# Layer A's normed queries turned in 32×32 blocks by VectorE, with a head every five slots

## The chip, the core and the metric

The kernel runs on one core of a Trainium2 chip. Its engines are TensorE (PE in the profile, with its weight loads as PEld), VectorE (DVE), ScalarE (ACT), GpSimd (POOL) and SyncE (SP, which only issues DMAs). Each works through its own instructions in a fixed order and waits at an instruction until the semaphores it needs have come. The metric is the device time of one execution in microseconds (us), the median of several runs.

## What is computed

A two-layer encoder over 256 tokens of width 2048: layer A has banded softmax attention with normed queries and keys, layer B another attention; both have a cross-attention into 256 memory tokens, an output projection and an MLP. The change lies in layer A's projections and attention:

```python
xn = rms_norm(h, norm_attn[layer])
mem_n = rms_norm(mem, norm_mem[layer])
proj = xn @ w_in_a[layer]
q = rms_norm(split_heads(proj[..., :W_MAIN], N_HEADS_MAIN), qk_gain_a[layer, 0])
k = rms_norm(split_heads(proj[..., W_MAIN:2 * W_MAIN], N_HEADS_MAIN), qk_gain_a[layer, 1])
v = split_heads(proj[..., 2 * W_MAIN:3 * W_MAIN], N_HEADS_MAIN)
y_main = chunk_band_attention(q, k, v, rel_bias[layer])
qm = proj[..., 3 * W_MAIN:]
y_mem = memory_attention(split_heads(qm, N_HEADS_MEM), mem_n, w_mem_kv[layer],
                         qk_gain_mem[layer, 0], qk_gain_mem[layer, 1])
```

There are 12 banded heads and 4 memory heads, each 128 wide. A query or key is divided by its own root mean square, and multiplied by a gain that has one value per feature of the head. The scores are products of queries and keys, so a gain of the queries may as well be put on the keys.

## The kernel before

**Numbers in halves.** Every weight is split into a high part that TensorE can multiply fast (`hi`, made by ScalarE, L173) and the remainder (`lo`, made by VectorE, L176). A *unit* is 1024 columns of weights for 128 partitions: one DMA into `raw`, one `hi`, one `lo`. There are 6 buffers for `raw`, 4 for `hi` and 5 for `lo`, and `weights()` prepares units up to three ahead of the one TensorE uses. A new `hi` can therefore begin when TensorE has finished the unit four before it.

**Groups and slots.** In layer A `tokens_major` computes a block of 512 output columns for all 256 tokens: 8 units of 12 matmuls, into two PSUM banks (one for each half of the tokens). After every unit it calls `slot()`, which lets each active side job take one step, up to its next `yield`. The matmuls and transposes a side job issues there stand in TensorE's order between two units, because TensorE's instructions are kept in the order in which the program writes them. On the other engines the build's scheduler decides the order. So TensorE's place for a head's work is fixed by slots, and what VectorE does before that head's work is fixed by the scheduler.

**The order of the groups.** Layer A has ten groups: `qm` (the four memory heads' queries), then three times `q`, `k`, `v` for four banded heads each, called here q0, k0, v0, q1, … v2. That is 80 slots; with slot 0 at the end of `qm`, q0 ends at slot 8, k0 at 16, v0 at 24, q1 at 32, k1 at 40, v1 at 48, q2 at 56, k2 at 64, v2 at 72.

**Norming and turning** (`normed_heads`, L556). For each of a group's two halves: ScalarE squares the bank (`sqw`, L561), VectorE sums the squares (`ss`, L563) and scales them (`msq`, L567), GpSimd takes the power −1/2 (`sroot`, L571), VectorE multiplies the bank by it (`qn`, L573). `qn` has tokens on the partitions, but the scores need the head's features there. So after `wait` slots TensorE transposes four blocks of 128×128 against an identity into the PSUM tile `tp`, and ScalarE copies `tp` to the destination with the gain as its scale (L592); one half in each of two slots. All queries and keys go this way.

**Heads.** `queue_side` puts a head in a line that is first in, first out: a head starts no earlier than 5 slots after it was queued, and no earlier than `gap` slots after the head before it. Memory heads have a gap of 4, banded heads of 2 (the last four: 1). A memory head (`mem_head`, L641) does its score matmuls `s`, the maximum (`nmax`, L651), the exponentials (`p`, L657) and their reciprocal sums (`rs`) in its first slot's step; four slots later it transposes `p` on TensorE into `tp`, ScalarE copies that to `pt`, and two slots later comes `yp`, the product with the values. A banded head (`band_head`, L667) loads its bias in its first slot, does `s`, `ns` (VectorE, L684), the exponentials (ScalarE, L692), `rs` (L697) and the scaling of `ns` (VectorE, L617, 128 and then 256 columns) in the second, transposes `ns` two slots after that, and multiplies by the values one slot later. `split_psum` then writes `y` (ScalarE L473, VectorE L474).

With these gaps the memory heads start at slots 5, 9, 13, 17, and the banded heads at 21, 23, 25, 27, then 45, 47, 49, 51, then 69 to 72. A banded head's `s` comes one slot after its start.

**Stages.** Memory keys and values come first, then layer A's ten groups (about 90 to 345 us), the output projection, the MLP, and layer B.

Of the kernel before, what the change touches and what calls it, by code (L numbers as in the profile page):

```python
# [9 lines left out]
F32 = mybir.dt.float32  # L10
# [6 lines left out]
P = 128  # L17
# [88 lines left out]
def trunk(  # L106
# [161 lines left out]
    def start_side(g):  # L268
        active.append(g)

    def queue_side(g, gap):
        waiting.append((g, gap, clock["slot"] + 5))

    def slot():
        clock["slot"] += 1
# [179 lines left out]
    def pin(ins, pinned=True):  # L455

        if pinned:
            tc.keep_in_program_order(ins)
# [88 lines left out]
    def inverse_square(acc, name):  # L547
# [5 lines left out]
        nc.vector.reciprocal(r2[:], r2[:])  # L553
        return r2

    def normed_heads(banks, eps_ms, gain, dst, wait=2):  # L556


        def half(m):
            sq = wide.tile([P, 512], F32, name="sqw", tag="wide")  # L560
            nc.scalar.activation(sq[:], banks[m][:], AF.Square)  # L561
            ss = tiny.tile([P, 4], F32, name="ss", tag="t4", bufs=8)
            nc.vector.tensor_reduce(  # L563
                ss[:], sq[:].rearrange("p (h d) -> p h d", d=HD), AX.X, ALU.add
            )
            ms = tiny.tile([P, 4], F32, name="msq", tag="t4", bufs=8)
            nc.vector.tensor_scalar(  # L567
                ms[:], ss[:], 1.0 / HD, eps_ms[:, 2 * m : 2 * m + 1], op0=ALU.mult, op1=ALU.add
            )
            s = tiny.tile([P, 4], F32, name="sroot", tag="t4", bufs=8)  # L570
            nc.gpsimd.tensor_tensor(s[:], ms[:], neg_half[:], op=ALU.pow)  # L571
            qn = wide.tile([P, 512], F32, name="qn", tag="wide")
            nc.vector.tensor_tensor(  # L573
                qn[:].rearrange("p (h d) -> p h d", d=HD),
                banks[m][:].rearrange("p (h d) -> p h d", d=HD),
                s[:].unsqueeze(2).to_broadcast([P, 4, HD]),
                op=ALU.mult,
            )
            return qn

        def side():
            qns = [half(0), half(1)]
            for _ in range(wait):
                yield
            for m in range(2):
                yield
                tp = ps_t.tile([P, 512], F32, name="tp", tag="t")
                for j in range(4):
                    nc.tensor.transpose(
                        tp[:, j * P : (j + 1) * P], qns[m][:, j * P : (j + 1) * P], ident[:]  # L590
                    )
                nc.scalar.activation(  # L592
                    dst.rearrange("p (h t) -> p h t", t=T)[:, :, m * P : (m + 1) * P],
                    tp[:].rearrange("p (h t) -> p h t", t=P),
                    AF.Copy,
                    scale=gain,
                )

        g = side()
        next(g)  # L600
        start_side(g)
# [288 lines left out]

    gq = const.tile([P, 3], F32, name="gq")

    def scale_gains():
        for i in range(3):
            g = sm[:, G_QK + 2 * i : G_QK + 2 * i + 1]
            pin(nc.vector.tensor_scalar_mul(gq[:, i : i + 1], g, QSCALE))

    later(scale_gains, 10)

# [12 lines left out]
    for l, mg in enumerate((mg0, mg1)):  # L912
        if l == 1:
            xg = new_act("xg")
            start_side(
                delayed(spaced(lambda kt: split_scaled(xg, kt, xs(kt), G_ATTN0, True), KT, 1), 4)
            )
        k_ = heads4(f"km{l}")
        km.append(k_)
        vm.append(heads4(f"vm{l}"))  # L920
        g = G_QK + 2 * (1 + l) + 1

        def keys(b, wait, k_=k_, g=g):

            late = 2 + wait
            later(lambda: normed_heads(b, mstat["em"], sm[:, g : g + 1], k_[:], late), wait)

        if l == 0:
            first_two(
                mg,  # L930
                lambda b: later(lambda: value_heads(b, mstat["r"], vm[0]), 5),
                lambda b: keys(b, 2),
            )
            xs = load_tokens(x_t, "xc", nc.sync)
            x_sq = square_sum("x_sq")
            start_side(delayed(all_squares(x_sq, lambda c: xs(4 * c, 4), 1, True), 10))
        else:
            tokens_major(mg, lambda b: keys(b, 0))
            tokens_major(mg, lambda b: value_heads(b, mstat["r"], vm[1]))
# [269 lines left out]

    start_side(x_stat_side())  # L1210
    qm = heads4("qm0")
    tokens_major(xg, lambda b: normed_heads(b, mstat["xem"], gq[:, 1:2], qm[:]))
    y = new_act("y0")
    for j in range(NM):
        queue_side(mem_head(qm, km[0], vm[0], j, y, 2), 4)

    for i in range(3):
        q_, k_, v_ = heads4(f"q{i}"), heads4(f"k{i}"), heads4(f"v{i}")
        tokens_major(xg, lambda b: normed_heads(b, mstat["xem"], gq[:, 0:1], q_[:]))
        tokens_major(  # L1220
            xg, lambda b: normed_heads(b, mstat["xem"], sm[:, G_QK + 1 : G_QK + 2], k_[:])
        )
        ready = {}
        for j in range(4):
            queue_side(band_head(q_, k_, v_, j, 4 * i + j, y, ready, 1), 2 if i < 2 else 1)

        def values(b, v_=v_, ready=ready):
            value_heads(b, mstat["xr"], v_)
# [153 lines left out]
```

## Time and profile before

| | |
|---|---|
| median of 3 runs | 2172.17 us (2171.57 to 2173.44) |
| the profiled execution | 2173.2 us, of which its span 2171.3 us |
| granted TensorE clock | 0.999 |
| DVE busy over the span | 1639.0 us (75%) |
| ACT busy over the span | 1196.6 us (55%) |
| POOL busy over the span | 324.4 us (15%) |
| HBM read and written | 190 GB/s over the span |

The page counts an engine as busy while an instruction of it runs, so a share near 100% means that it hardly ever stood still. It does not say that its work was all needed. The chain of waits is followed back from the last instruction: an engine's share of it is the part of the span that a cut on that engine could shorten.

### The profile page before, as it was taken

The numbers are of one execution on the slowest core, as the hardware profiler recorded it, in microseconds if no ns is written. First come the engines' busy times: TensorE is split into PE (matmuls) and PEld (weight loads), VectorE is DVE, ScalarE is ACT, GpSimd is POOL, SyncE is SP. The second block draws the span as 40 slices with busy tenths as digits, with TensorE's granted clock in tenths as the row PEclk, the third lists the DMA queues.
The fourth block names the chain that finished last, engine by engine and source line by source line (L and its number), as shares of the span: only waits on it lengthen the run. The fifth ranks groups of instructions, "written<-read, shape, count | busy, mean of one in ns | idle before, by whom it ended". The sixth has DMA issues, their size and how long they took to land.

```text
span 2171.3 us, 30203 instructions
## 1 busy us (share of the span) xinstructions
PE 2164.1 (100%) x11123; PEld 1856.6 (86%) x11123; DVE 1639.0 (75%) x2239; ACT 1196.6 (55%) x1680; POOL 324.4 (15%) x349
## 2 busy tenths in 40 slices
PE   9999999999999999999999999999999999999999
PEld 8888888888888888888878888888888888888887
DVE  7765555677977987997876556567797798799796
ACT  7645545555655565555545447655565556555553
POOL 0010102621001001001041112253100100100100
PEclk9999999999999999999999999999999999999999
DMA  9655656665765765666666654455676567667664
GB/s 331 194 173 162 180 173 196 187 193 168 210 214 172 210 210 184 192 214 192 200 177 186 182 192 140 130 185 184 181 207 216 172 198 221 191 178 221 187 182 155
DMA packets 213315, 414.64 MB, mean 191 GB/s; under 512 B 13232, under 2 KB 144304, under 8 KB 213168
## 3 DMA queue, kind: packets, MB, share of 16 engines
q1 hardware_dynamic: 212592, 410.63, 62.3%
q8 instruction: 87, 1.43, 0.3%
q10 hardware_dynamic: 576, 2.10, 0.3%
q14 instruction: 60, 0.49, 0.1%
HBM read 410.58 MB, written 2.10 MB: 190 GB/s over the span
## 4 chain that ended last, share of the span: by engine, by line
PE 99%; DVE 0%; DMA 0%; ACT 0%; issue 0%; ACTq 0%
PE acc L77 94%; PE accs L77 1%; PE tp L77 1%; PE yp L77 1%; PE s L77 1%; PE z L77 1%; DMA raw<-in_w_o 0%; PE cold L77 0%; ACT hi L173 0%; DVE lo L250 0%; DVE h L983 0%; DVE lo L176 0%; DVE kvx L465 0%; ACT hi L249 0%; PE stat L77 0%
## 5 line engine op out<-in xcount | busy, mean ns | idle before, releaser
L176 DVE TENSOR_TENSOR lo<-raw,hi 128x1024 fp32r<-128x1024 f32 (+1 forms) x524 | 644.4, 1237 | 357.6 <-ACT hi L173 239.5
L173 ACT CAST hi<-raw 128x1024 fp32r<-128x1024 f32 (+1 forms) x524 | 546.7, 1045 | 380.0 <-PE acc L77 307.5
L77 PE MATMUL acc<-hi,hid 128*128 128x512 f32 x1474 | 482.4, 390 | 0.0
L77 PE MATMUL acc<-mlpx,hi 128*128 128x512 f32 x2048 | 472.6, 390 | 0.0
L77 PEld LDWEIGHTS acc<-mlpx,hi 128*128 128x128 f32 x2048 | 382.0, 188 | 77.8
L77 PEld LDWEIGHTS acc<-hi,hid 128*128 128x128 f32 x1474 | 277.4, 188 | 57.7
L77 PE MATMUL acc<-lo,hid 128*128 128x512 f32 x737 | 287.4, 390 | 0.0
L1080 POOL TENSOR_TENSOR hid<-upsq,hid 128x256 fp32r<-128x256 f32 x128 | 122.2, 963 | 1086.2 <-ACT hid L1079 1086.2
L227 ACT CAST hi<-raw 128x1024 fp32r<-128x1024 f32 x204 | 192.0, 946 | 132.8 <-PE acc L77 57.2
L77 PEld LDWEIGHTS acc<-mlpx,lo 128*128 128x128 f32 x2048 | 250.6, 192 | 2.8
L77 PE MATMUL acc<-mlpx,lo 128*128 128x256 f32 x2048 | 252.0, 283 | 0.0
L228 DVE TENSOR_TENSOR lo<-raw,hi 128x1024 fp32r<-128x1024 f32 x204 | 222.8, 1107 | 29.3 <-ACT hi L227 27.7
L249 ACT CAST hi<-raw 128x1024 fp32r<-128x1024 f32 x146 | 154.0, 1055 | 127.5 <-PE acc L77 104.0
L77 PE MATMUL acc<-hi,xg 128*128 128x512 f32 x640 | 210.5, 399 | 0.0
L250 DVE TENSOR_TENSOR lo<-raw,hi 128x1024 fp32r<-128x1024 f32 x146 | 178.4, 1222 | 16.3 <-ACT hi L249 15.6
L77 PEld LDWEIGHTS acc<-lo,hid 128*128 128x128 f32 x737 | 138.7, 188 | 28.7
L77 PEld LDWEIGHTS acc<-hi,xg 128*128 128x128 f32 x640 | 120.2, 188 | 24.6
L451 ACT COPY low<-acc 128x256 f32<-128x256 f32 x188 | 69.1, 368 | 112.5 <-PE acc L77 112.2
L77 PE MATMUL acc<-lo,xg 128*128 128x512 f32 x320 | 124.7, 390 | 0.0
L77 PE MATMUL acc<-y,hi 128*128 128x512 f32 x512 | 119.9, 391 | 0.0
L77 PEld LDWEIGHTS acc<-y,hi 128*128 128x128 f32 x512 | 95.0, 188 | 19.1
L1079 ACT CAST hid<-upsq 128x256 fp32r<-128x256 f32 x128 | 51.9, 406 | 77.1 <-DVE upsq L1078 77.1
(200 smaller groups left out, 2570.5 us busy)
## 6 DMA issues: line engine op xcount, KB each, us to landing
raw<-in_w_up SPq DMA_DIRECT2D x256, 512.0 KB, 4.4
raw<-in_w_down SPq DMA_DIRECT2D x256, 512.0 KB, 5.6
raw<-in_w_in SPq DMA_DIRECT2D x80, 512.0 KB, 3.6
raw<-in_w_o SPq DMA_DIRECT2D x64, 512.0 KB, 3.9
raw<-in_w_mem SPq DMA_DIRECT2D x28, 512.0 KB, 6.2
raw<-in_w_kv_v SPq DMA_DIRECT2D x24, 512.0 KB, 3.7
raw<-in_w_kv_k SPq DMA_DIRECT2D x24, 512.0 KB, 4.0
raw<-in_w_q SPq DMA_DIRECT2D x24, 512.0 KB, 4.2
```

Of the source, the lines that this page charges most:

```text
L77: return self._tc.keep_in_program_order(fn(*args, **kwargs))
L173: nc.scalar.copy(hi[:, :n], raw[:, :n])
L176: nc.vector.tensor_tensor(lo, raw, hi.bitcast(F32), op=ALU.subtract)
L227: nc.scalar.copy(hi4, src)
L228: nc.vector.tensor_tensor(lo4, src, hi4.bitcast(F32), op=ALU.subtract)
L249: nc.scalar.copy(hi4, turned)
L250: nc.vector.tensor_tensor(lo4, turned, hi4.bitcast(F32), op=ALU.subtract)
L451: nc.scalar.copy(low[:], bank[:, T:])
L1079: nc.scalar.copy(hid[:, f, :T], a[:])
L1080: nc.gpsimd.tensor_tensor(hid[:, f, T:], a[:], hid[:, f, :T].bitcast(F32), op=ALU.subtract)
```

## The change

Layer A's `qm`, q0, q1 and q2 are no longer transposed by TensorE. A new function `quadrants` lets VectorE turn them in blocks of 32×32: each instruction takes 32 partitions and one block of 32 columns of each of the four heads (32×4×32 elements), turns every block in itself and writes it to the 32 partitions where it belongs. A half needs 16 of them, four in each of four slots, so a group needs 32 over 8 slots. `wait` goes from 2 to 1 for these groups, so their first turn is issued in the slot in which the group ends. The gain of the queries is no longer a scale of the copy; it is multiplied into the keys' gain (`gk`, made from `gq` and the keys' gain by two small VectorE instructions at the start), which the keys' copy uses as before. Keys, and layer B's queries, are still transposed by TensorE.

The heads are spread: memory heads have a gap of 5 and start no earlier than 11 slots after they are queued (`first`), the first eight banded heads have a gap of 5; the last four keep 1. By the rule above, memory heads now start at slots 11, 16, 21, 26, banded heads at 31, 36, 41, 46, then 51, 56, 61, 66, then 69 to 72.

```diff
-    def queue_side(g, gap):
-        waiting.append((g, gap, clock["slot"] + 5))
+    def queue_side(g, gap, first=5):
+        waiting.append((g, gap, clock["slot"] + first))
...
+    def quadrants(qn, m, dst):
+
+
+        src = qn.rearrange("p (h d) -> p h d", d=HD)
+        dst = dst.rearrange("p (h t) -> p h t", t=T)
+        for a in range(4):
+            for b in range(4):
+                nc.vector.transpose(
+                    dst[32 * b : 32 * b + 32, :, m * P + 32 * a : m * P + 32 * a + 32],
+                    src[32 * a : 32 * a + 32, :, 32 * b : 32 * b + 32],
+                )
+            yield
+
     def normed_heads(banks, eps_ms, gain, dst, wait=2):
...
             for _ in range(wait):
                 yield
+            if gain is None:
+                for m in range(2):
+                    yield from quadrants(qns[m][:], m, dst)
+                return
             for m in range(2):
...
+    gk = const.tile([P, 2], F32, name="gk")
+
     def scale_gains():
         for i in range(3):
             g = sm[:, G_QK + 2 * i : G_QK + 2 * i + 1]
             pin(nc.vector.tensor_scalar_mul(gq[:, i : i + 1], g, QSCALE))
+        for i in range(2):
+            k = sm[:, G_QK + 2 * i + 1 : G_QK + 2 * i + 2]
+            pin(nc.vector.tensor_tensor(gk[:, i : i + 1], gq[:, i : i + 1], k, op=ALU.mult))
...
-            later(lambda: normed_heads(b, mstat["em"], sm[:, g : g + 1], k_[:], late), wait)
+            gain = gk[:, 1:2] if k_ is km[0] else sm[:, g : g + 1]
+            later(lambda: normed_heads(b, mstat["em"], gain, k_[:], late), wait)
...
-    tokens_major(xg, lambda b: normed_heads(b, mstat["xem"], gq[:, 1:2], qm[:]))
+    tokens_major(xg, lambda b: normed_heads(b, mstat["xem"], None, qm[:], 1))
     y = new_act("y0")
     for j in range(NM):
-        queue_side(mem_head(qm, km[0], vm[0], j, y, 2), 4)
+        queue_side(mem_head(qm, km[0], vm[0], j, y, 2), 5, 11)
...
-        tokens_major(xg, lambda b: normed_heads(b, mstat["xem"], gq[:, 0:1], q_[:]))
-        tokens_major(
-            xg, lambda b: normed_heads(b, mstat["xem"], sm[:, G_QK + 1 : G_QK + 2], k_[:])
-        )
+        tokens_major(xg, lambda b: normed_heads(b, mstat["xem"], None, q_[:], 1))
+        tokens_major(xg, lambda b: normed_heads(b, mstat["xem"], gk[:, 0:1], k_[:]))
         ready = {}
         for j in range(4):
-            queue_side(band_head(q_, k_, v_, j, 4 * i + j, y, ready, 1), 2 if i < 2 else 1)
+            queue_side(band_head(q_, k_, v_, j, 4 * i + j, y, ready, 1), 5 if i < 2 else 1)
```

The change adds lines ahead of most of the code, so the same instruction has a higher line number: by 14 in the first part of `normed_heads` (`ss` goes from L563 to L577, `qn` from L573 to L587), by 18 behind it (`ns` from L684 to L702, the scaling from L617 to L635). The turns themselves are L563 of the changed kernel. The scheduler has put VectorE's instructions in an order that the diff does not show, at three places that matter below.

The first place is VectorE at the end of q1 (slot 32). Before, these rows stood there: the norming of q1's two halves, with splits of weights (`lo`) between them, and no head near it:

```order
L563 TENSOR_REDUCE ss<-sqw 128x4
L567 TENSOR_SCALAR msq<-ss,em_x 128x4
L176 TENSOR_TENSOR lo_2066<-raw_2064,hi_2065 128x1024
L573 TENSOR_TENSOR qn<-acc,sroot 128x512
L563 TENSOR_REDUCE ss<-sqw 128x4
L567 TENSOR_SCALAR msq<-ss,em_x 128x4
L176 TENSOR_TENSOR lo_2084<-raw_2082,hi_2083 128x1024
L573 TENSOR_TENSOR qn<-acc,sroot 128x512
```

In the changed program the same place begins like this (`y` is the last memory head's output; `q_1787` is q1):

```order
L577 TENSOR_REDUCE ss<-sqw 128x4
L581 TENSOR_SCALAR msq<-ss,em_x 128x4
L176 TENSOR_TENSOR lo_2016<-raw_2014,hi_2015 128x1024
L474 TENSOR_TENSOR y_1168<-yp,y_1168 128x256
L587 TENSOR_TENSOR qn<-acc,sroot 128x512
L577 TENSOR_REDUCE ss<-sqw 128x4
L563 STREAM_TRANSPOSE q_1787<-qn 32x4x32 x9
L581 TENSOR_SCALAR msq<-ss,em_x 128x4
```

It goes on without a gap, with the first banded head of q0 in the middle of it (`ns` and `nmax` in four ISA rows, then `rs`, and the scaling of `ns` as the last row):

```order
L563 STREAM_TRANSPOSE q_1787<-qn 32x4x32 x7
L176 TENSOR_TENSOR lo_2040<-raw_2038,hi_2039 128x1024
L587 TENSOR_TENSOR qn<-acc,sroot 128x512
L702 ISA ns,nmax<-s,bias 128x128
L702 ISA nmax 128x1
L702 ISA ns,nmax<-s,bias 128x256
L702 ISA nmax 128x1
L176 TENSOR_TENSOR lo_2068<-raw_2066,hi_2067 128x1024
L563 STREAM_TRANSPOSE q_1787<-qn 32x4x32 x12
L715 RECIPROCAL rs<-sums 128x2
L563 STREAM_TRANSPOSE q_1787<-qn 32x4x32 x4
L635 TENSOR_SCALAR ns<-ns,rs 128x128
```

What moved: q1's first sixteen turns stand ahead of the head's `ns`, and its other sixteen ahead of the scaling of `ns`, which is what the head's transposes on TensorE need.

The second place is VectorE at the end of q2 (slot 56; `q_2452` is q2). The first rows are as at q1 but without the `y`; from the ninth turn on:

```order
L563 STREAM_TRANSPOSE q_2452<-qn 32x4x32 x9
L581 TENSOR_SCALAR msq<-ss,em_x 128x4
L176 TENSOR_TENSOR lo_2705<-raw_2703,hi_2704 128x1024
L563 STREAM_TRANSPOSE q_2452<-qn 32x4x32 x7
L587 TENSOR_TENSOR qn<-acc,sroot 128x512
L702 ISA ns,nmax<-s,bias 128x128
```

Behind the `ns` of 256 columns stand there, one after the other, a split (`lo_2729`), twelve turns, another split (`lo_2757`), `rs`, four turns and the scaling. Again a banded head (its `s` in slot 57) lies between the halves of the turns; before, no head was near q2's end.

On TensorE the head's score matmuls at the first place stand directly behind the last matmul of q1 and the last memory head's `yp`; two units, 24 matmuls, follow before the head's transposes:

```order
L77 MATMUL acc<-lo_1891,xg 128x512
L77 MATMUL acc<-hi_1890,xg 128x512
L77 MATMUL yp<-pt,vm_184 128x256 x2
L77 MATMUL s<-k_1170,q_1169 128x128
L77 MATMUL s<-k_1170,q_1169 128x256
L77 MATMUL acc<-hi_1908,xg 128x512
```

Before, nothing but q1's own four transposes stood between the units there (two slots later).

The third place is ScalarE at the end of k2 (slot 64), where a banded head's transposes fall in the same slot; `pt` is the copy that the head's `yp` needs one slot later:

```order
L575 ACTIVATE sqw<-acc 128x512
L173 CAST hi_2912<-raw_2911 128x1024
L575 ACTIVATE sqw<-acc 128x512
L173 CAST hi_2935<-raw_2934 128x1024
L649 COPY pt<-tp 128x384
L473 CAST y_1168<-yp 128x256
```

What moved: `pt` now stands behind a split, `hi_2935`, whose buffer is that of the unit which TensorE works on just before the head's `yp`. Before, no head was at this point.

## The prediction

> **What bounds the kernel now.** I read the page's busy times first, then the chain of waits, then the busy time of each engine by stage, then single pieces of layer A in order of time.
>
> ```profile
> PE 2164.1 (100%) x11123; PEld 1856.6 (86%) x11123; DVE 1639.0 (75%) x2239; ACT 1196.6 (55%) x1680; POOL 324.4 (15%) x349
> PE 99%; DVE 0%; DMA 0%; ACT 0%; issue 0%; ACTq 0%
> core 0: us, PE busy (x) PEld busy (x) DVE busy (x) ACT busy (x) POOL busy (x), PEclk, DMA share, GB/s
> 144.00:220.00 76.00, 76.00 (x365) 63.32 (x364) 43.57 (x80) 39.81 (x73) 5.50 (x7) 1.00 0.55 161
> 220.00:290.00 70.00, 70.00 (x330) 58.19 (x329) 39.56 (x66) 35.77 (x56) 6.26 (x6) 1.00 0.59 176
> ```
>
> TensorE never stands still in layer A (76.00 of 76 us, 70.00 of 70), and the chain is 99% TensorE. So each microsecond taken off TensorE here is won, each wait of TensorE is lost, and VectorE has room on the mean: 43.57 of 76 us. A mean says nothing about whether one head's work comes in time, though, and TensorE takes its instructions in a fixed order.
>
> **What TensorE is spared.** The chain of waits around q1 and k1, with each piece's start, length and what ran:
>
> ```profile
> 229.26 0.44 PE tp L77 x4
> 229.70 2.77 PE acc L77 x12
> 232.47 0.44 PE tp L77 x4
> 232.90 19.09 PE acc L77 x84
> ```
>
> A unit of 12 matmuls with nothing between takes 2.73 us (12/84 of the 19.09 in the last row). From one `tp` to the next are 3.21 us, so four transposes cost 0.48 us. Eight such blocks go (two in each of qm, q0, q1, q2): 3.9 us. One of them stands directly beside other fp32 work, where the switch to fp32 and back is shared, and the wider gaps move up to nine `s` blocks away from beside a `tp`; a switch is worth 0.04 us (0.48 less the 0.44 of the block itself), so that gives back up to 0.4. Net gain: **3.5 us**. ScalarE's eight copies of `tp` go too, but ScalarE is not on the chain: nothing. The two small multiplications for `gk` fall into the memory stage, hidden by TensorE's lead there: nothing, and if that cover failed, 0.3 us.
>
> **What VectorE is given.** 128 turns. The trace has no such instruction; nearest are VectorE's rows with 128 columns, and how close two instructions follow each other shows in the head's own piece (the timeline of VectorE, columns start, length):
>
> ```profile
> L617 DVE TENSOR_SCALAR ns<-ns,rs 128x128 f32<-128x128 f32 x12 | 3.4, 287 | 0.4
> L617 DVE TENSOR_SCALAR ns<-ns,rs 128x256 f32<-128x256 f32 x12 | 4.2, 347 | 0.0
> 196.92 0.29 DVE L684 CUSTOM_DVE_ANT_0 ns<-s,bias 128x128 f32<-128x128 f32 x1 [1.94 <-PE s L77]
> 197.13 0.08 DVE L684 DVE_READ_ACCUMULATOR2_ANT nmax<- 128x1 f32 x1
> 197.13 0.42 DVE L684 CUSTOM_DVE_ANT_0 ns<-s,bias 128x256 f32<-128x256 f32 x1
> 197.48 0.08 DVE L684 DVE_READ_ACCUMULATOR2_ANT nmax<- 128x1 f32 x1
> 197.59 1.23 DVE L176 TENSOR_TENSOR lo<-raw,hi 128x1024 fp32r<-128x1024 f32 x1
> 198.85 0.17 DVE L697 RECIPROCAL rs<-sums 128x2 f32<-128x2 f32 x1
> 199.05 0.55 DVE L617 TENSOR_SCALAR ns<-ns,rs 128x128 f32<-128x128 f32 x2
> ```
>
> A 128-column instruction takes 0.287 us by itself. The last row holds both scalings in 0.55 us where 0.287 and 0.347 make 0.634: the second starts 0.08 before the first ends. And `rs` to the scaling that needs it goes 0.20 for 0.17: a start held until the end adds 0.03. So a turn costs t = 0.20 us if it overlaps its forerunner, 0.29 to 0.32 if it waits for its end. By the columns alone (0.42 less 0.29 for 128) it would be 0.13; at the other end, if a turn is as dear as 256 columns, 0.42. I take **0.30**: every overlap in the trace is between instructions that cover all 128 partitions, none shows one whose output begins at other partitions than its forerunner's, as each turn's does.
>
> The Trainium skill bears on this choice ("VectorE: DVE Perf Modes", section "Two Vector instructions with no wait between them"): an instruction whose output starts in another group of 32 partitions than the last one is held until all earlier ones have finished. By that rule 0.20 is out; no run here shows it yet. The sum below is +12.0 us with overlap and +18.4 without. The same page's "The three transpose paths" gives 311 ns for a 128×128 turn in 32×32 blocks of 2-byte numbers, and its rules for authors leave 128×128 transposes to TensorE where the result may go to PSUM; t = 0.31 would add 0.6 to the sum.
>
> **Where it meets a head: the end of q1.** The undisturbed norming there, from the timeline:
>
> ```profile
> 223.17 0.60 ACT L561 ACTIVATE sqw<-acc 128x512 f32<-128x512 f32 x1 [1.36 <-PE acc L77]
> 223.81 0.69 DVE L563 TENSOR_REDUCE ss<-sqw 128x4 f32<-128x512 f32 x1 [0.67 <-ACT sqw L561]
> 224.53 0.23 DVE L567 TENSOR_SCALAR msq<-ss,em_x 128x4 f32<-128x4 f32 x1
> 224.94 1.23 DVE L176 TENSOR_TENSOR lo<-raw,hi 128x1024 fp32r<-128x1024 f32 x1 [0.18 <-ACT hi L173]
> 226.10 0.68 DVE L573 TENSOR_TENSOR qn<-acc,sroot 128x512 f32<-128x512 f32 x1
> 226.70 0.67 DVE L563 TENSOR_REDUCE ss<-sqw 128x4 f32<-128x512 f32 x1
> 227.41 0.23 DVE L567 TENSOR_SCALAR msq<-ss,em_x 128x4 f32<-128x4 f32 x1
> 227.78 1.98 POOL L571 TENSOR_TENSOR sroot<-msq,neg_half 128x4 f32<-128x4 f32 x1 [1.87 <-DVE msq L567]
> ```
>
> I count from the start of `sqw` (0). `qn` comes at 2.93, `ss` 0.60 later. In the changed order a `y` stands ahead of `qn` (it delays the next instruction by 0.34: 256 columns, 0.42 as in the row of `ns`, less 0.08), so `ss` is at 3.87 and over at 4.46. Then, each with the delay it gives the next: 9t, `msq` 0.15, 7t, `lo` 1.15, the second `qn` 0.60, the two `ns` 0.50, `lo` 1.15, 12t, `rs` 0.08, 4t, and the first scaling 0.29. That ends at 8.38 + 32t. The second `qn` waits for nothing more: its power on GpSimd (1.98) is done while seven turns and the split run (3.2).
>
> When does TensorE want it? Two places of the chain, a memory head's `yp` and a banded head from `s` to `tp`:
>
> ```profile
> 192.26 0.86 PE yp L77 x4
> 263.84 0.66 PE s L77 x4
> 264.50 5.47 PE acc L77 x24
> 269.97 0.33 PE tp L77 x3
> ```
>
> The group's last matmul ends about 0.4 us after `sqw` starts (the first half's bank is done three matmuls early), `yp` takes 0.86, and from `s` to `tp` are 6.13: due 7.4 us after `sqw`. So TensorE waits 0.9 + 32t there, **10.5 us** at 0.30, and everything behind that `tp` on TensorE waits with it. Before, VectorE's part took from 196.92 to 199.60 (the rows above), with the 0.66 of `s` 3.4 us of the 6.13, so there was no wait.
>
> **The end of q2.** Here no `y` stands in the way, `ss` is over at 4.12, and then come 9t, 0.15, 1.15, 7t, 0.60, 0.50, 1.15, 12t, the second split 1.15, 0.08, 4t and 0.29: 9.19 + 32t. The head's `s` comes a unit later and without the `yp`: due 0.4 + 2.73 + 6.13 = 9.3 us after `sqw`. TensorE waits 32t − 0.1, **9.5 us**. At both places the second transpose needs the 256-column scaling as well, another 0.16: **0.3 us** together.
>
> **The end of k2.** ScalarE's rows that matter:
>
> ```profile
> ACT hi L173 <- PE acc L77: 307.5, 336, 5.3
> L173 ACT CAST hi<-raw 128x1024 fp32r<-128x1024 f32 x81 | 85.1, 1050 | 108.3 <-PE acc L77 68.9 <-issue 32.5 <-DMA raw<-in_w_o 2.6
> L631 ACT COPY pt<-tp x20: 473/484/582, 145.4 to 1372.2; 128x384 f32<-128x384 f32 x12, 128x512 f32<-128x512 f32 x8
> ```
>
> A split (`hi`) waits for TensorE in most cases, 336 times: for the buffer of the unit four before. Behind the change `hi_2935` stands ahead of `pt`, and the unit it waits for is the last one before the head's `yp`. So `yp` comes due when that split only begins, and waits for 1.05 + 0.48 and the hand-over: **1.6 us**.
>
> **The sum.** −3.5 + 10.5 + 9.5 + 0.3 + 1.6 = **+18.4 us**. The profiled execution took 2173.2 us (its span 2171.3 and 1.9 around it), so it would take 2191.6; the median of the runs shown, 2172.2, is 1.0 below it, so I predict **2190.6 us**. By the other values of t: +7.6 at 0.13, +12.0 at 0.20, +19.7 at 0.32.
>
> **The splits of weights** are not what TensorE waits for at 0.30. A unit's `hi` begins when the unit four before it ends, and `hi` and `lo` take 2.3 us of the 8.2 that the three units between take: 5.9 spare. VectorE is furthest behind in the turns of qm, where with the rows of its order the fourth split is over 9.6 + 31t after `sqw` (18.9) and due at 19.7.
>
> **Rivals.**
> - *The turns overlap.* For it: VectorE's rows above overlap wherever the second needs nothing of the first. Against: they write to other partitions each time. At t = 0.20 to 0.23 the two waits are 4 to 6 us shorter together: about 2184.2. Chance 0.15.
> - *A turn is dearer than its 128 columns*, because a block of 32 must be read before it can be written. Then a third and a fourth place begin to wait. The first memory head has its `s` three units after the end of q0, and its `tp` four slots later:
>
> ```profile
> 132.61 0.86 PE s L77 x4
> 133.47 10.93 PE acc L77 x48
> ```
>
>   That makes 11.8 from `s` to `tp`, due 0.4 + 8.2 + 11.8 = 20.4 us after q0's `sqw`; VectorE's rows there add up to 10.5 + 32t, so it waits from t = 0.31 on, and the fourth split in qm from 0.33. At t = 0.40: 13.7 + 12.7 + 2.9 + 2.4 + 1.9 − 3.5 = +30, so 2202; at the upper end, 0.42, 2205. Chance 0.14.
> - *Not slower: the turns run four at a time.* The four turns of a step read the same 32 partitions and write to four different quarters. If VectorE, whose other rows use all 128 partitions, ran such quarters beside each other, t would be 0.29/4 = 0.07 and the waits 3.2 and 2.1: −3.5 + 3.2 + 2.1 + 1.9 = +3.7, so 2175.9, within 0.2%. It decides at t = 0.08. Against it: one engine's instructions overlap by 0.08 in every row here, never by more. Chance 0.07.
> - *The heads are not held up*, since VectorE reaches their work early. That needs the 32 turns to cost less than nothing in the sum at q1 (0.9 stays at t = 0), unless GpSimd's power or `sqw` came sooner than in the rows above. What is left would be −3.5 us, 2168.7, still within 0.2%. Chance 0.02.
>
> **How the numbers follow.** The forecast, t between 0.26 and 0.34, has 0.62: 2188 to 2194. A measurement of this kernel can tell about 0.2%, 4.3 us, from no change. The range of 8 in 10 takes in the forecast, the overlapping turns and the lower part of the dearer ones: 2183 to 2199; the four at a time, the heads not held up and the dear end are left out. Slower by over 0.2% are the first three cases, 0.91. Within 0.2% are the two last, 0.08, since their times lie 3.5 us either side of before; 0.01 is left for faster, which would need more than the 3.9 us that the eight blocks hold.
>
> **What the next profile would show.** Right: a row of 128 turns with a mean near 0.3 us that do not overlap; two long waits of TensorE, each about 10 us, at a `tp` from `ns`, put down to VectorE's scaling, near 225 and 310 us; a wait of 1.6 us at a `yp` for ScalarE's `pt`; TensorE's transposes of `qn` down from 80 to 48. Wrong: TensorE at 100% through layer A, or its waits at `acc` for `lo` instead of at `tp`. What would undo the forecast most easily is the price of a turn: 0.01 us of it is 0.64 us of the result.

## The result, and the profile after

The changed kernel takes **2197.66 us** (median of four runs, 2197.50 to 2198.11), the kernel before on the same chip 2171.99 us (four runs, 2171.57 to 2173.44). The ratio is 1.0116, with a 95% interval of 1.0104 to 1.0128: slower, as predicted, but by 25.7 us where 18.4 were forecast. The time lies inside the range (2183 to 2199), 7.1 us above the predicted 2190.6. The profiled execution took 2197.5 us, its span 2195.8.

The page after, busy time of each engine, then the shares of the chain that ended last:

```profile
PE 2164.5 (99%) x11091; PEld 1855.4 (84%) x11091; DVE 1676.1 (76%) x2369; ACT 1192.2 (54%) x1672; POOL 321.8 (15%) x349
PE 95%; DVE 3%; issue 1%; ACT 0%; POOL 0%; POOLq 0%
```

TensorE has 32 instructions fewer and is busy as long as before (2164.1): part of its work has become slower. VectorE, at 0% of the chain before, now has 3% of it, some 65 us (the chain goes back through VectorE's own instructions behind each wait, so this is more than TensorE stood). The view of TensorE's waits says where it comes in (columns: who waits for whom, us in total, times, longest):

```profile
PE tp L77 <- DVE ns L635: 21.5, 2, 11.3
PE tp L77 <- DVE p L635: 1.9, 1, 1.9
PE tp L77 <- DVE h L1007: 1.9, 2, 1.1
PE yp L77 <- ACT pt L649: 1.6, 1, 1.6
```

Two waits for VectorE's scaling of `ns`, 11.3 and 10.2 us, stand at the ends of q1 and q2; one for a memory head's scaled `p`, and one at a `yp` for ScalarE. (The row with `h` is in layer B, and stood there before with 2.7 us in two times.) What a turn costs shows in the turns by themselves (min, median and max in ns, first and last start):

```profile
L563 DVE STREAM_TRANSPOSE q<-qn x96: 289/303/308, 144.5 to 325.5; 32x128 f32<-32x128 f32 x96
L563 DVE STREAM_TRANSPOSE qm<-qn x32: 290/303/308, 121.3 to 136.6; 32x128 f32<-32x128 f32 x32
```

And this is VectorE during the wait at q1's end, in order of time (start, length, what ran):

```profile
224.87 2.21 DVE L563 STREAM_TRANSPOSE q<-qn 32x128 f32<-32x128 f32 x7
227.11 1.23 DVE L176 TENSOR_TENSOR lo<-raw,hi 128x1024 fp32r<-128x1024 f32 x1
228.25 0.68 DVE L587 TENSOR_TENSOR qn<-acc,sroot 128x512 f32<-128x512 f32 x1
...
229.41 1.22 DVE L176 TENSOR_TENSOR lo<-raw,hi 128x1024 fp32r<-128x1024 f32 x1
230.54 3.76 DVE L563 STREAM_TRANSPOSE q<-qn 32x128 f32<-32x128 f32 x12
234.34 0.17 DVE L715 RECIPROCAL rs<-sums 128x2 f32<-128x2 f32 x1
234.53 1.26 DVE L563 STREAM_TRANSPOSE q<-qn 32x128 f32<-32x128 f32 x4
235.83 0.55 DVE L635 TENSOR_SCALAR ns<-ns,rs 128x128 f32<-128x128 f32 x2
```

Twelve turns in a row take 3.76 us: eleven steps of 0.315 and one turn of 0.303. So a turn starts about 0.013 us after the end of the one before it, and no two of these overlap. The reciprocal `rs` could have been followed by the scaling at once; four turns stand between them, and twelve ahead of `rs`.

The third thing to see is the clock. The view of stretches gives, for each, its length, the busy time of PE, PEld, DVE, ACT and POOL, and then TensorE's granted clock:

```profile
158.51:161.92 3.41, 1.49 (x10) 0.96 (x8) 3.34 (x8) 1.04 (x1) 0.00 (x0) 1.00 0.00 0
161.92:165.33 3.41, 3.41 (x11) 2.73 (x9) 3.03 (x3) 0.59 (x1) 0.00 (x0) 0.50 0.78 214
165.33:168.74 3.41, 3.41 (x16) 2.83 (x16) 2.23 (x4) 2.14 (x3) 1.01 (x1) 1.00 0.97 360
230.18:240.42 10.24, 4.16 (x12) 3.40 (x13) 5.91 (x20) 0.48 (x1) 0.14 (x1) 0.50 0.36 100
236.20:240.20 4.00, 3.94 (x11) 3.28 (x12) 0.18 (x1) 0.48 (x1) 0.00 (x0) 0.50 0.00 0
240.42:243.83 3.41, 3.41 (x18) 2.85 (x17) 1.20 (x2) 1.32 (x2) 0.00 (x0) 1.00 0.00 0
318.93:329.17 10.24, 2.86 (x9) 2.39 (x10) 7.21 (x21) 0.63 (x3) 0.14 (x1) 0.50 0.38 117
329.17:332.58 3.41, 3.41 (x18) 2.84 (x16) 0.49 (x1) 1.32 (x2) 0.00 (x0) 1.00 0.00 0
```

Behind three of the waits the clock is 0.50 (the fifth row is a part of the fourth). While TensorE waits that costs nothing; but it has 3.41, 4.16 and 2.86 us of work in these stretches, done at half speed. Half of it is lost: 1.7 + 2.1 + 1.4 = **5.2 us**. The timeline of TensorE shows the same from close by, at the end of the wait:

```profile
236.26 0.87 PE L77 MATMUL tp<-ident,ns 128*128 128x128 f32 x3 [11.29 <-DVE ns L635]
...
237.79 1.05 PE L77 MATMUL acc<-hi,xg 128*128 128x512 f32 x2
238.64 0.63 PE L77 MATMUL acc<-lo,xg 128*128 128x512 f32 x1
...
345.22 0.62 PE L77 MATMUL acc<-hi,xg 128*128 128x512 f32 x2
```

Two matmuls of 512 columns take 1.05 us at 237.79, and 0.62 us in the last row, at full clock.

**The account.** From layer A's first matmul to layer B's first transpose TensorE takes 1000.60 us before (95.66 to 1096.26) and 1027.77 us after (95.38 to 1123.15): 27.2 more. That is 21.5 + 1.9 + 1.6 = 25.0 of waits, 5.2 of half clock, less the transposes that are gone; with 3.6 for those (an experiment below measures it) it comes to 26.6, and 0.6 is left over, for which no row was found. From layer B's first transpose to the end, the change is 2.4 us *shorter* (1069.15 against 1071.60), in code that it does not touch. That needed an experiment too. The medians are further apart than the two profiled executions (25.7 against 24.3 us); the section on layer B shows why.

### The profile page after: what moved, and what is told of

Its sections match the earlier page's. It is cut to its first block, busy times and chain, and to the rows that moved or that the text cites. A ratio compares the mean times of both kernels' runs of the same rounds, so it can differ in the third digit from the quotient of the medians.

```text
span 2195.8 us, 30244 instructions
## 1 busy us (share of the span) xinstructions
PE 2164.5 (99%) x11091; PEld 1855.4 (84%) x11091; DVE 1676.1 (76%) x2369; ACT 1192.2 (54%) x1672; POOL 321.8 (15%) x349
## 4 chain that ended last, share of the span: by engine, by line
PE 95%; DVE 3%; issue 1%; ACT 0%; POOL 0%; POOLq 0%
PE acc L77 91%; DVE q L563 1%; PE accs L77 1%; PE yp L77 1%; DVE lo L176 1%; PE tp L77 1%; PE z L77 1%; PE s L77 1%; DVE qm L563 0%; ACT hi L173 0%; DVE qn L587 0%; PE cold L77 0%; DVE ss L577 0%; DVE lo L250 0%; DVE h L1007 0%
```

## The experiments

Three theories had to be told apart. **A**: the turns stand in VectorE's order ahead of work that TensorE waits for, at three places, and each long wait is paid a second time as half clock. **B**: the spread of the heads costs the time, whatever is done with the queries. **C**: VectorE's or TensorE's total load is what counts. All ratios below are to the kernel before, run on the same chip. Its medians on the chips used are 2172.0 to 2173.6 us, so where two kernels ran on different chips, their times alone do not tell differences under 2 us.

### The spread alone

The kernel before with the changed gaps, and the queries still transposed by TensorE:

```diff
-    def queue_side(g, gap):
+    def queue_side(g, gap, first=5):
...
-        queue_side(mem_head(qm, km[0], vm[0], j, y, 2), 4)
+        queue_side(mem_head(qm, km[0], vm[0], j, y, 2), 5, 11)
...
-            queue_side(band_head(q_, k_, v_, j, 4 * i + j, y, ready, 1), 2 if i < 2 else 1)
+            queue_side(band_head(q_, k_, v_, j, 4 * i + j, y, ready, 1), 5 if i < 2 else 1)
```

> The kernel before with only the change's new gaps and first starts of the heads; all queries still transposed by TensorE, no turns on VectorE. Theory (a head's VectorE work stands behind q1's and q2's turns and norming in VectorE's order): the turns' part of the waits, 64 x 0.316 = 20.2 us, is gone; at q1's end 2.9 us of wait stay, because the head's ns still stands behind the second qn, which waits for GpSimd; at most 1.4 at q2 and 1.6 at k2's yp: 2175 to 2181 us. Rival (the turns load VectorE as a whole): nothing is left, 2172. Rival (the wider gaps themselves cost the time): above 2190.

Measured: 2180.39 us (four runs, 2179.49 to 2181.97), ratio 1.0037 (1.0023 to 1.0051). Its waits:

```profile
PE tp L77 <- DVE ns L617: 2.9, 1, 2.9
PE yp L77 <- ACT pt L631: 1.6, 1, 1.6
PE tp L77 <- ACT q L592: 1.3, 1, 1.3
PE tp L77 <- ACT pt L631: 0.6, 1, 0.6
```

The first of them is followed by half clock, like the long waits of the changed kernel:

```profile
226.96:230.37 3.41, 3.03 (x9) 2.57 (x10) 0.00 (x0) 1.01 (x2) 0.14 (x1) 0.50 0.34 129
```

So B holds in part: putting heads at the ends of q1 and q2 costs 8 us even without turns, 6.4 of waits and 1.5 of half clock. Not all of it is in the changed kernel's 25.7. The wait of 1.6 at the `yp` is there in full: it belongs to the gaps. The 1.3, for a copy of transposed queries, and the 0.6 are not there. The long waits do not belong to the gaps: 2.9 us here where the changed kernel has 21.5.

### The turns alone

All turns, but no banded head beside them: memory heads from slot 12 on, one every two slots, and the banded heads' gaps as before.

```diff
-        queue_side(mem_head(qm, km[0], vm[0], j, y, 2), 5, 11)
+        queue_side(mem_head(qm, km[0], vm[0], j, y, 2), 2, 12)
...
-            queue_side(band_head(q_, k_, v_, j, 4 * i + j, y, ready, 1), 5 if i < 2 else 1)
+            queue_side(band_head(q_, k_, v_, j, 4 * i + j, y, ready, 1), (2, 2, 1)[i])
```

> The changed kernel with only the heads' starts moved: memory heads from slot 12 on with a gap of 2, banded heads with the gap of 2 of before, so that no head's work falls into the turns of q1 or q2. All 128 turns stay. Theory: both long waits go, and with them the slow clock behind them; what is left is the 3.5 us that TensorE is spared, less about 0.8 of small waits: 2167 to 2171 us. Rival (the turns load VectorE as a whole): 2190 or more, since all turns are there. Rival (wider gaps): 2168 too.

Measured: 2168.0 us (eleven runs, 2167.45 to 2168.72), ratio 0.9979 (0.9970 to 0.9988), faster than both kernels. VectorE does the same 128 turns of 0.303 us, and all that TensorE waits for in layer A is this:

```profile
PE tp L77 <- ACT pt L649: 0.9, 1, 0.9
```

That is against C: the load is the changed kernel's, and the loss is gone. To see what the turns are worth there, a control has the same places for the heads, but leaves the transposes to TensorE:

```diff
...
-        queue_side(mem_head(qm, km[0], vm[0], j, y, 2), 4)
+        queue_side(mem_head(qm, km[0], vm[0], j, y, 2), 2, 12)
```

> The kernel before with only the memory heads moved to where the version with all turns and no heads beside them has them (first slot 12, gap 2): TensorE still transposes all queries. It tells what the turns alone are worth there. Theory A (a group turned by VectorE beside no head spares TensorE its transposes and costs nothing): this kernel is 3.5 us slower than that version, about 2171.5 us, whether or not it also loses the 2.5 us at the start of layer B. Rival (that version gained by the memory heads' places and by the order at layer B's start, the turns being worth nothing): the two are equal within 1 us, about 2168.

> The version with all turns, memory heads from slot 12 with a gap of 2 and banded gaps of 2, 2, 1, once more, beside the one above on the same chip: 2167.5 to 2168.5 us, ratio to before 0.998.

Measured beside each other, eleven runs each: the control 2171.47 us (2171.08 to 2172.23), ratio 0.9995 (0.9986 to 1.0004); the version with turns 2167.91 us (2167.41 to 2168.42), ratio 0.9981 (0.9972 to 0.9990). The runs' ranges do not meet. Their difference is **3.6 us**: eight blocks of four transposes, the 3.5 of the prediction's first term. Layer A alone, from its first matmul to layer B's first transpose, shows the same in the two profiled executions: 1001.12 and 997.56 us.

### TensorE kept busy while it waits

The changed kernel, with matmuls that nobody uses in the two long waits:

```diff
+        for _ in range({0: 44, 5: 40}.get(head, 0)):
+            nc.tensor.matmul(tp[:], neg_tri_r[:], xg[:, 0, :], start=True, stop=True)
```

> The changed kernel with TensorE kept at work in its two long waits: 44 matmuls of 512 columns (0.227 us each, 10.0 us) ahead of the transposes of the first slot of q1's head, and 40 (9.1 us) ahead of those of q2's. Nothing uses their results. The turns on VectorE, their order and the ends of the two waits stay as they are. Theory A (a long wait is paid twice, once as the wait and once as a slow clock behind it, 1.4 + 1.7 us at these two places, and 2.1 us for the other two): the half-clock stretches behind the two waits go, and the time is 2194 to 2195 us, below the change's 2197.7, though TensorE does 19 us more work. Theory B (only the waits cost): 2197 to 2198 us. Theory C (the slow clock has to do with something else than the standing): the stretches stay and the time is 2197 us or more.

Measured: 2194.09 us (four runs, 2193.31 to 2194.20), ratio 1.0097 (1.0082 to 1.0112). With 19 us *more* work for TensorE it is 3.6 us faster than the changed kernel (by the ratios 4.1), and the two ranges of runs do not meet. The stretch behind the first wait, to be set beside the one above:

```profile
224.90:235.90 11.00, 10.04 (x44) 7.81 (x42) 10.60 (x33) 1.89 (x5) 0.98 (x2) 1.00 0.41 107
235.90:239.90 4.00, 3.97 (x20) 3.27 (x21) 0.23 (x1) 0.89 (x2) 0.00 (x0) 1.00 0.00 0
```

VectorE is as long about its work as before (10.60 of 11 us), so the end of the wait has not moved. But the clock behind it is 1.00, and in 4 us TensorE does 20 instructions where it did 11 at half clock (the row from 236.20 above). The slow clock is thus a price of standing still, and separate from the wait. No stretch of this execution's layer A has half clock, so all of the 5.2 us should be won. From layer A's first matmul to layer B's first transpose 4.7 are (1023.09 us against 1027.77); the span is only 3.4 shorter, because layer A begins 1.3 us later here (96.68 against 95.38).

### Who stands ahead of whom

The changed kernel with the turns and the heads' scalings kept in the order in which the program writes them, so that the scheduler may no longer put later turns ahead of a scaling:

```diff
-                nc.vector.transpose(
+                pin(nc.vector.transpose(
...
-            nc.vector.tensor_scalar_mul(p[:, lo:hi], p[:, lo:hi], rs[:, m : m + 1])
+            pin(nc.vector.tensor_scalar_mul(p[:, lo:hi], p[:, lo:hi], rs[:, m : m + 1]))
```

> The changed kernel with the same heads, slots and turns; only VectorE's order is another: the turns and the scaling of p and ns are kept in the order in which the program writes them, so that a head's scaling no longer stands behind all 32 turns. Theory: the wait at q1 falls from 11.4 to about 5 us, that at q2 from 10.4 to about 6, so 2182 to 2188 us. Rivals (load of VectorE, wider gaps): 2197, since neither is changed.

Measured: 2186.15 us (four runs, 2185.76 to 2186.51), ratio 1.0063 (1.0048 to 1.0079). The waits, with the row of the memory head at the end:

```profile
PE tp L77 <- DVE ns L635: 11.7, 2, 6.7
...
PE yp L77 <- ACT pt L649: 1.6, 1, 1.6
...
PE tp L77 <- DVE p L635: 0.3, 1, 0.3
```

Neither turns nor heads have moved in the program, only their order on VectorE, and 11.5 us of the 25.7 are gone. The other way round, TensorE may ask later:

```diff
-            queue_side(band_head(q_, k_, v_, j, 4 * i + j, y, ready, 1), 5 if i < 2 else 1)
+            queue_side(band_head(q_, k_, v_, j, 4 * i + j, y, ready, 2 if i < 2 else 1), 5 if i < 2 else 1)
```

> The changed kernel with one more slot between the scaled probabilities and their transposes in the heads of q0 and q1's bands, so that TensorE asks for them some 10 us of its work later in the stream, with nothing else moved and all gaps as in the change. Theory A (the wait is VectorE's scaling, late behind the turns, and a later question takes that much off): by a replay of the trace with the new order about 8 us of wait at q1's end and 2 at q2's instead of 11.5 and 10.4, and with less slow clock behind them 2184 to 2190 us. Rival (VectorE is late throughout these stages, and what is asked later is late by as much): 2196 us or more.

Measured: 2188.82 us (four runs, 2188.11 to 2190.39), ratio 1.0075 (1.0058 to 1.0092).

```profile
PE tp L77 <- DVE ns L635: 10.8, 2, 8.3
PE yp L77 <- DVE y L474: 1.9, 1, 1.9
PE tp L77 <- DVE p L635: 1.9, 1, 1.9
```

8.3 and 2.6 us where 8 and 2 were expected: the later question takes off 3 us at q1's end and 8 at q2's, and a part comes back, as the wait of 1.9 at a `yp` and one of 1.2 at a `tp` for a copy by ScalarE. The rival, that VectorE is late throughout, would have left the time at 2196 or more.

### What a turn costs

A first version put the two halves' turns of one place behind each other, without fixing their order:

```diff
...
         for a in range(4):
             for b in range(4):
-                nc.vector.transpose(
+                for m in range(2):
+                    nc.vector.transpose(
...
-            yield
+                if b % 2 == 1:
+                    yield
```

> The changed kernel with the turns of both halves taken in pairs: two turns in a row read the same 32 partitions and write to the same 32. If a turn waits for its forerunner's end only where the partitions change, the second of each pair starts some 0.08 to 0.11 us earlier, the mean step from turn to turn falls from 0.316 to about 0.27, the two long waits by 1.3 to 1.5 us each, and the time to 2194 to 2195 us. If every turn waits for its forerunner's end, whatever the partitions, the step stays at 0.316 and the time at 2197.7.

Measured: 2196.99 us (two runs, 2196.49 and 2197.50), ratio 1.0113 (1.0094 to 1.0131), and a step of 0.316 as before. This says nothing of the turns: the second half's `qn` comes later, so the scheduler had issued the first half's sixteen turns before any of the second half, and no pair stood together. The next run fixed the order (`turn` is one pinned turn; `g` counts the groups from qm), on the version with no banded head beside the turns, and has four forms in one program:

```diff
...
+        steps = [(m, a, b) for m in range(2) for a in range(4) for b in range(4)]
+        if g == 1:
+            steps.sort(key=lambda s: (s[0], s[2], s[1]))
+        if g == 2:
+            steps.sort(key=lambda s: s[1:])
+        for n, (m, a, b) in enumerate(steps):
+            if g == 3:
+                turn(m, a, b, slice(0, 2))
+                turn(m, a, b, slice(2, 4))
+            else:
+                turn(m, a, b)
...
```

> The changed kernel with the earlier heads and wider gaps undone, and the turns pinned in program order in four forms: the first memory queries as in the change; q0 with the same output partitions four times in a row; q1 with the same input and output partitions twice in a row (the two halves of one place); q2 with each turn cut in two turns of two heads, 64 elements long, at the same place. In the change a turn takes 0.303 us and the next starts 0.316 us after it. Theory A (a turn is held by the one before it wherever it stands): the step is the turn's own time plus about 0.013 us in all four forms; the turns of 64 elements take about 0.18 us. Theory B (held where partitions change): the second turn at the same place starts about 0.08 us earlier, 0.24 us after the first, in q1, and in q0 too if the output partitions decide. The time is no test here (pinning 64 turns in q2 makes others late); about 2172 to 2176 us.

Measured in one run: 2170.35 us, below the 2172 to 2176 expected. Rows of VectorE's timeline, one for each form, in the order qm, q0, q1, q2:

```profile
124.01 1.25 DVE L566 STREAM_TRANSPOSE qm<-qn 32x128 f32<-32x128 f32 x4
147.86 1.26 DVE L566 STREAM_TRANSPOSE q<-qn 32x128 f32<-32x128 f32 x4
234.18 1.01 DVE L566 STREAM_TRANSPOSE q<-qn 32x128 f32<-32x128 f32 x4
300.21 1.49 DVE L566 STREAM_TRANSPOSE q<-qn 32x64 f32<-32x64 f32 x8
```

Four turns take 1.25 us when the output's partitions change from each to the next (qm), 1.26 when only the input's change (q0), and 1.01 when pairs keep both (q1). From start to start, the medians in q1 are 0.236 us from a turn to the other of its pair and 0.274 from there to the next pair, where qm and q0 have 0.316. In q2 the halved turns go 0.169 to the one at the same place and 0.207 to the next place. Theory B of this run holds: a turn overlaps its forerunner by 0.07 us where both begin at the same partitions, and is held until its end where either side changes. Halving a turn doesn't pay (0.376 for the two halves).

Does a cheaper turn shorten the wait? The pinned kernel once more, with pairs:

```diff
...
-                pin(nc.vector.transpose(
-                    dst[32 * b : 32 * b + 32, :, m * P + 32 * a : m * P + 32 * a + 32],
-                    src[32 * a : 32 * a + 32, :, 32 * b : 32 * b + 32],
-                ))
-            yield
+                for m in range(2):
+                    pin(nc.vector.transpose(
+                        dst[32 * b : 32 * b + 32, :, m * P + 32 * a : m * P + 32 * a + 32],
+                        srcs[m][32 * a : 32 * a + 32, :, 32 * b : 32 * b + 32],
+                    ))
+                if b % 2 == 1:
+                    yield
```

> The kernel with the changed gaps and with turns and scalings pinned in program order, but each turn followed by that of the other half at the same 32 input and the same 32 output partitions. Theory A (a turn's step is 0.316 us where its partitions differ from the turn before and 0.24 where both are the same, and each turn ahead of a scaling is paid in the wait): step 0.24 and 0.27 by turns, 0.255 in the mean where 0.316 was, and 1 to 2 us less than the 2186.15 us without the pairs, 2184 to 2185. Rival (the step belongs to the turn or the waits do not follow it): 2186 us.

Measured: 2183.78 us (four runs, 2182.97 to 2184.61), ratio 1.0053 (1.0039 to 1.0066), 2.4 us less than without the pairs on another chip, 2.2 by the ratios; a little more than expected. Steps of 0.236 and 0.273 us (medians), and 10.8 us of waits for `ns` instead of 11.7. A memory head's wait of 0.3 is gone too. Most of the rest is clock: the stretch of half clock at the first wait is 3.4 us here and 6.8 without the pairs, and TensorE works for 3.4 and 5.0 us of them, which is 0.8 us. Together that is 2.0 of the 2.1 us by which layer A is shorter (1013.26 us against 1015.40). How much of the 0.8 follows from the pairs, and how much from where the stretches begin, is not shown.

### The 2.4 us at the start of layer B

The kernel before, unchanged, profiled a second time:

> The kernel before, unchanged, in a second profiled execution. In the first one TensorE stands for 2.18 us at the start of layer B (tp<-ident,d, about 1111 us) and then has 3.4 us at a granted clock of 0.5; the changed kernels stand for 1.38 us there and keep their clock, which is 2.5 us to the change's credit. If that belongs to the program, this execution shows a gap above 2 us and the slow stretch at the same place again. If it belonged to one execution, the gap is about 1.4 us, there is no slow stretch, and the span is about 2.5 us shorter, 2169 us.

Span 2170.9 us. The same gap, in the timeline of TensorE, and the same clock behind it, in the view of stretches:

```profile
1108.19 0.60 PE L77 MATMUL tp<-ident,d 128*128 128x128 f32 x4
1110.71 0.66 PE L77 MATMUL tp<-ident,d 128*128 128x128 f32 x4 [1.92 <-DVE h L983]
```

```profile
1111.68:1115.10 3.42, 3.42 (x10) 2.65 (x9) 3.42 (x6) 0.91 (x2) 3.42 (x5) 0.50 0.50 153
1115.10:1118.00 2.90, 2.90 (x16) 2.41 (x15) 2.34 (x3) 1.97 (x3) 2.75 (x4) 1.00 0.00 0
```

So it belongs to the program before: two groups of transposes of `d` start 2.52 us apart, and 1.7 us more go to half clock. In every other kernel here the wait is at most 1.1 us (the longest in the row of `h` above), and the clock stays. Even the two kernels whose only change is the heads' places have lost it.

It is not another order of work: from layer B's first transposes on, TensorE, VectorE, ScalarE and GpSimd run the same instructions in the same order before and after. It is timing. A split of weights on ScalarE and VectorE stands just ahead of the wait, here in the kernel before (first execution) and in the changed kernel:

```profile
1103.20 1.05 ACT L249 CAST hi<-raw 128x1024 fp32r<-128x1024 f32 x1 [1.38 <-issue]
1104.28 1.74 DVE L250 TENSOR_TENSOR lo<-raw,hi 128x1024 fp32r<-128x1024 f32 x1 [0.76 <-ACT hi L249]
...
1129.80 1.05 ACT L249 CAST hi<-raw 128x1024 fp32r<-128x1024 f32 x1 [1.08 <-issue]
1130.89 1.23 DVE L250 TENSOR_TENSOR lo<-raw,hi 128x1024 fp32r<-128x1024 f32 x1 [0.47 <-ACT hi L249]
```

Counted from layer B's first transposes, the `hi` begins 0.29 us later before than after, and its `lo` takes 0.51 us longer: together the 0.8 by which the wait is longer. Why the `hi` begins later is open: the view names nothing that it waits for.

The second part, the half clock, is not paid in every execution. Over the three chips of these experiments the kernel before has 43 runs: 20 show a granted clock of 0.999 and take 2172.82 to 2174.28 us, 23 show 1.000 and take 2171.23 to 2172.59. The medians of the two groups are 1.5 us apart, about the 1.7 of the slow stretch. Both profiled executions above are of the first group. Three of the four runs behind the median of 2171.99 lie in the second group's times, and so the medians show little of the 2.4.

## Why the prediction was right in kind and too low

- **TensorE's gain, −3.5.** Right: 3.6 measured, by the control.
- **The price of a turn, t = 0.30.** Right in kind: no overlap, as chosen from the row of `rs`; the step is 0.316. The reason given, that each turn's output begins at other partitions than the last one's, is what the four forms show, and they add that a change of the input's partitions does the same. The rule that was weighed (the Trainium skill, "VectorE: DVE Perf Modes", section "Two Vector instructions with no wait between them") says both, and the traces agree: 0.316 us where either side changes, 0.236 where neither does.
- **The two waits, 0.9 + 32t and 32t − 0.1.** Right: 11.3 and 10.2 us, where the formulas give 11.0 and 10.0 at 0.316. The places, the engine and the rows between are those of the trace above. 1.0 us of the miss is t, 0.5 the formulas, of which 0.1 is a slip in the sum: 8.38 less the 0.4, 0.86 and 6.13 until the wait is 1.0, not 0.9. (Two more slips change nothing: at t = 0.13 the sum gives +7.5 instead of +7.6, and the last two chances make 0.09 instead of 0.08.)
- **The second transposes, 0.3.** It did not come as a wait: there are only two waits for `ns`, and both are those of a first transpose.
- **The `yp` at k2's end, 1.6.** Right, 1.6; and the spread alone has it too.
- **The first memory head.** Named among the rivals as waiting from t = 0.31; t came out 0.316, and the wait is 1.9 us. By that rival's sum the wait would be 0.2 us at this price, so the sum was 1.7 us short as well. It takes `qn` at 2.9 us after `sqw`, as in the undisturbed norming; here it comes at 4.4 (143.34, with `sqw` at 138.91), because VectorE is still at splits when the squares are there and then stands 0.9 us for GpSimd's power. The forecast stood 0.01 us of t away from this place and counted it at nothing. The fourth split in qm, the other half of that rival, made no wait.
- **The clock.** This is the term that failed by being absent. The sum took a wait at its length; three of the four were also paid in half clock behind them, 5.2 us. It is the largest term of the miss. Filling the waits gave back 3.6 us by the medians and 4.7 in layer A. The profile of before held the sign: its granted clock was 0.999, not 1, and one stretch of it, behind the longest wait in the program, ran at 0.50.
- **Layer B, −2.4.** Absent as well, on the other side. The changed kernel loses a wait of the kernel before in code far from the edit, whose order is the same; why is open.

Together: 18.4 forecast, +1.0 for t, +0.5 for the formulas, +1.9 for the memory head, +5.2 for the clock and −2.4 in layer B are 24.6 us. The two profiled executions are 24.3 apart, the medians 25.7, since most of the runs before do not pay the half clock in layer B.

So the places, the engine and the form of the waits were forecast, and the total was not. That it still lies inside the range is luck in part: the upper end was given to dearer turns, and half clock, which the prediction does not have, filled it.

Of the rivals, the overlapping turns fall (0.303 us each, 0.316 from start to start), and with them four turns at a time. That heads are not held up holds only when they are put elsewhere: 2167.9 us with the banded heads out of the way, where 2168.7 was given for that case. Of the 4.1 us that this kernel gains on its chip 3.6 are the turns'; the control has the rest too.

## What to carry to other kernels

Work moved to an engine with room on the mean is free only where nothing with a deadline stands behind it in that engine's order; here the same 128 turns win 3.6 us where no banded head is near, and lose 17 where they stand ahead of a scaling that TensorE waits for (2197.66 us against 2180.39 with the same places of the heads and no turns). So read the order on the receiving engine, and either move the consumers out of the way or keep the scheduler from putting bulk work ahead of them. And price a wait of TensorE of about 2 us or more at its length plus the half clock that may follow it, 1.7 us for every 3.41 us of work at that clock.

## What was not expected of the hardware

**The clock falls in steps of 3.41 us, on a grid.** In the changed kernel the slow stretches begin at 161.92, 230.18 and 318.93 us: 20 and 26 times 3.413 us apart. Each begins at the end of one such interval in which TensorE stood for most of the time, and lasts as many intervals as stood so. In the interval from 158.51 to 161.92 TensorE was busy for 1.49 us, so it stood for 1.92, and the next one is at half clock. The same wait in the kernel with the filled waits, 1.91 us long, falls across a border of its grid (counted back from the slow stretch at its end), with 1.49 us ahead of the border and 0.42 behind it, and no slow interval follows:

```profile
158.90:162.31 3.41, 1.92 (x9) 1.26 (x7) 3.25 (x10) 1.38 (x2) 0.00 (x0) 1.00 0.03 12
162.31:165.73 3.42, 3.00 (x15) 2.53 (x16) 3.42 (x6) 0.74 (x2) 0.00 (x0) 1.00 0.63 172
```

So the same wait may cost 1.9 us in one execution and 3.6 in another. Even a wait of 2.56 us, in the run where TensorE asks later, cost no clock: a border at 321.73 cut it in 1.57 and 1.00 (320.16 to 322.73). The Trainium skill ("TensorE: Matmul & The Clock Gate", section "What's actually happening") describes a free-running window of 3413 ns, and the grid agrees with it. Its section "Why this matters for your kernels" advises no gaps over about 3 us; in these runs 1.92 us within one window was enough to slow the next one. 1.80 us was not: the first long wait begins at 224.97 (11.29 before 236.26), 1.80 ahead of the border at 226.77, and the window from there still has the full clock:

```profile
226.77:230.18 3.41, 0.00 (x0) 0.00 (x0) 3.38 (x8) 0.99 (x4) 0.00 (x0) 1.00 0.18 47
```

**A turn's price hangs on its neighbour**: 0.236 us behind a turn at the same partitions, 0.316 behind one at others, though the two turns' own records differ by less, 0.26 us for the second of a pair and 0.30 for any other.
